# Slot ids fetched one block earlier, and a narrow block's rows turned in the last two steps of the block ahead

## The chip, the core and the metric

The kernel runs on one core of one Trainium2 chip. Its engines run side by side, each with a queue of its own: TensorE (PE: matrix products, and transposes written as products with the identity), VectorE (DVE), ScalarE (ACT), GpSimd (POOL, which here issues the indirect transfers) and SyncE (SP, which issues the plain loads). The metric is the device time of one execution in microseconds (us); less is better.

## The reference, cut to what matters

A layer first mixes 2048 tokens of width 1024 and normalises them; that part is not touched. Then comes a mixture of experts: every token picks a group and two of its eight experts, out of 32 in all. The changed code computes this (biases and the sorting are left out):

```python
def hier_moe(t, ...):                                    # t: (2048, 1024)
    g_val, g_idx = top_k(softmax(t @ rg_w), 1)
    e_val, e_idx = top_k(in_group(t @ re_w, g_idx), 2)
    weights = g_val * softmax(e_val)
    for each expert e:
        xb = the rows of t that chose e                  # gathered by slot id
        hid = silu(xb @ w1[e]) * (xb @ w3[e])            # 1024 -> 512
        y[rows of xb] += weights * (hid @ w2[e])         # 512 -> 1024
```

After it a second layer norm writes the output.

## The kernel before

The span has three stages: the mixer up to 1350 us, the experts from there to 2161.5 us, and the last norm. The router writes, for each expert, a list of slots into `idxD` in device memory: a slot holds a token's row number and its weight. An expert `e` owns `LE` slots there. `u2D` holds the rows to gather, `accD` the sum that the outputs are added to.

**Blocks.** The experts are ranked by size and worked off in 33 blocks. Block 0 holds 128 rows of the largest. Then wide blocks (`Wide`, 144 to 224 rows, odd numbers 1 to 27) alternate with narrow ones (`Block`, 80 to 128 rows, even numbers 2 to 28), and blocks 29 to 32 are four more narrow ones. A wide block has its rows in two halves. All products of 32-bit numbers are made as three products of a high and a low part.

**Rows of a block.** `gather` first loads the slots into a small tile `ix` (SP's queue, L1322), then has POOL fetch the token rows into `X` by them (an indirect transfer, L1324). `X` has three buffers, `ix` eight. `turned` (L1330) transposes four columns of 128 of `X` on TensorE into a PSUM tile `ptx`, of which there are two; `split_rows` then makes the high part on ScalarE (L1334) and the low part on VectorE (L1335), as `xw` (wide) or `xx` (narrow). A narrow block takes two such turns, a wide one four.

**Weights.** A piece of 512 KB is loaded by SP into one of eight buffers `raw` (L1307); `split` makes `whi` on ScalarE (L1314) and `wlo` on VectorE (L1315). A piece's buffer is free again, and the next load can be issued, when its `wlo` is done. `pump(m)` does up to m splits and issues the loads that follow. Each expert has eight pieces for the up products and four for the down products.

**Order.** Everything is issued in the order of the code, and each engine takes its own part of it in that order. Block t goes through four steps `s_`: its up products (L1395 to L1397 narrow, L1452 and L1453 wide), turns of block t + 1 (a wide one in each step, a narrow one in steps 0 and 2), two splits, and in step 0 `prepare(t + 2)`. `finish` is a block's down products (L1341 to L1343) and `put`, which scales the result on VectorE (`y`, L1350) and has POOL add it to `accD` (L1351). It comes in step 1 of the next block for a narrow one; a wide block finishes its first half at its own end, its second half at the end of the next block.

Of the kernel before, what the change touches and what calls it, by code (L numbers as in the profile page):

```python
# [10 lines left out]
I32 = mybir.dt.int32  # L11
# [63 lines left out]
def hymba_kernel(ctx, tc, xT, ctxT, x, small, rows, ada_w, w_in, gate_w, w_out, router_w, w1, w3, w2, out):  # L75
# [606 lines left out]
    slots = []  # L682
# [62 lines left out]
    for si in range(len(slots), 3, -1):  # L745
        a, b, c, d = slots[si - 4:si]
        turn = si == len(slots) or slots[si][0] != d[0] or (si - 4 > 0 and slots[si - 5][0] != a[0])
# [157 lines left out]
    with ExitStack() as st:  # L905
# [204 lines left out]
        def place(i):  # L1110
# [5 lines left out]
            sl = fs.tile([128, 2], F32, name="sl")  # L1116
            dve.tensor_reduce(sl, ho, axis=AX.X, op=ALU.add)
            dve.scalar_tensor_tensor(dest[:, i, :], ee, float(LE), sl, op0=ALU.mult, op1=ALU.add)
# [10 lines left out]
        def choose():  # L1129
# [11 lines left out]
            sp.dma_start(lead_ix, idxD[bass.ds(e * LE, 128), :])  # L1141
            X = upool.tile([128, D], F32, name="X0", tag="wr", bufs=2)
            pool.indirect_dma_start(out=X, out_offset=None, in_=u2D, in_offset=bass.IndirectOffsetOnAxis(ap=lead_ix[:, 0:1], axis=0))
            return e, X

        def turn_lead(X):
            pts = []
# [140 lines left out]
    with ExitStack() as st:  # L1288
# [5 lines left out]
        ex = st.enter_context(tc.tile_pool(name="ex", bufs=2))  # L1294
# [21 lines left out]
            k = 4 if n < 8 else 2  # L1316
            return [t.rearrange("p (k c) -> p k c", k=k) for t in (hi, lo)]

        def gather(row, n):

            ix = ex.tile([128, 2], I32, name="ix", tag="ix", bufs=8)
            sp.dma_start(ix[:n], idxD[bass.ds(row, n), :])  # L1322
            X = ex.tile([128, D], F32, name="X", tag="X", bufs=3)
            pool.indirect_dma_start(out=X[:n], out_offset=None, in_=u2D, in_offset=bass.IndirectOffsetOnAxis(ap=ix[:n, 0:1], axis=0))  # L1324
            return ix, X

        def turned(X, n, k0):
            pt = psT.tile([128, 4, 128], F32, name="ptx", tag="pt")
            for k in range(4):
                pe.transpose(pt[:, k, :n], X[:n, 128 * (k0 + k):128 * (k0 + k) + 128], ident[:n, :n])  # L1330
            return pt[:, :, :n]

        def split_rows(xh, xl, pt):
            act.copy(xh, pt)  # L1334
            dve.tensor_sub(xl, pt, xh.bitcast(F32))  # L1335
# [9 lines left out]
        def put(py, ix, n):  # L1345

            y = ex.tile([128, D], F32, name="y", tag="y")
            for nh in range(2):
                s = slice(512 * nh, 512 * nh + 512)
                dve.scalar_tensor_tensor(y[:n, s], py[nh][:n], ix[:n, 1:2].bitcast(F32), g2[:n, s], op0=ALU.mult, op1=ALU.mult)  # L1350
            pool.indirect_dma_start(out=accD, out_offset=bass.IndirectOffsetOnAxis(ap=ix[:n, 0:1], axis=0), in_=y[:n], in_offset=None, compute_op=ALU.add)  # L1351
# [4 lines left out]
        class Block:  # L1356
# [3 lines left out]
            def __init__(self, row, n, weights, slot):  # L1360
                self.row, self.n, self.w, self.slot = row, n, weights, slot

            def gather(self):
                self.ix, self.X = gather(self.row, self.n)

            def places(self):
                x = ex.tile([128, KC, 2, 128], F32R, name="xx", tag=self.slot, bufs=1)
# [11 lines left out]
            def turn(self, i):  # L1379
                if i == 0:  # L1380
                    self.places()
                k0 = 4 * i
                split_rows(self.xh[:, k0:k0 + 4, :], self.xl[:, k0:k0 + 4, :], turned(self.X, self.n, k0))
# [32 lines left out]
            def put(self, part=0):  # L1416
                put(self.py, self.ix, self.n)
# [3 lines left out]
        class Wide:  # L1421
# [5 lines left out]
            def __init__(self, row, n, weights, slot):  # L1427
                self.row, self.n, self.m, self.w, self.slot = row, n, n // 2, weights, slot

            def gather(self):  # L1430
                self.src = [gather(self.row + self.m * a, self.m) for a in range(2)]

            def turn(self, i):
                n, m = self.n, self.m
                if i == 0:
                    self.x = ex.tile([128, KC, 2, n], F32R, name="xw", tag=self.slot, bufs=1)
                a, k0 = i // 2, 4 * (i % 2)
                s = slice(m * a, m * a + m)
                split_rows(self.x[:, k0:k0 + 4, 0, s], self.x[:, k0:k0 + 4, 1, s], turned(self.src[a][1], m, k0))

            def up(self, s, kk):

# [29 lines left out]
                down(self.hh[:, k, s], self.hl[:, k, s], self.w[8 + k], k, self.py, self.m)  # L1472

            def put(self, part):
                put(self.py, self.src[part][0], self.m)

        SP = (mybir.EngineType.SP,)
        SPP = (mybir.EngineType.SP, mybir.EngineType.Pool)
# [17 lines left out]
        nb = len(blocks)  # L1496
        wide = [n > 128 for _, _, n, _ in blocks] + [False]

        def reg(s_):
            if s_ not in regs:  # L1500
                regs[s_] = nc.values_load(etab[0:1, sched[s_]:sched[s_] + 1], engines=SP, min_val=0, max_val=31)
            return regs[s_]
# [27 lines left out]
        if True:  # L1530
            B = []
            rest = overflow()

            def prepare(t):
                if t < nb:
                    s_, o, n, _ = blocks[t]
                    slot = "xw" if wide[t] or (not wide[t - 1] and B[t - 1].slot == "xs") else "xs"
                    B.append((Wide if wide[t] else Block)(reg(s_) * LE + o, n, weights[s_], slot))
                    B[t].gather()

            def finish(t, part):
                for k in range(4):
                    while 8 + k not in B[t].w:
                        pump(1)
                    B[t].down(k, part)
                    if blocks[t][3] and part == B[t].parts - 1:
                        state["down"] += 1
                    pump(1)
                B[t].put(part)

            def turn(t, i):
                if t < nb and i < B[t].turns:
                    B[t].turn(i)

            def used(t, i):
                if blocks[t][3]:
                    state["up"] += 2

            def late(t):
                if t == nb // 2:  # L1560
                    sp.dma_start(l2b, rows[0:1, 4096 + 3 * D:4096 + 4 * D].to_broadcast([128, D]))


            fetch_to(2)
            B.append(Block(reg(0) * LE, 128, weights[0], "xs"))
            prepare(1)
            prepare(2)
            fetch_to(NRAW)
            B[0].lead(lead_ix, lead_pt)
            pump(4)  # L1570
            for t in range(nb):
                for s_ in range(4):
                    while 2 * s_ + 1 not in B[t].w:
                        pump(1)
                    if wide[t]:
                        for kk in range(4):
                            B[t].up(s_, kk)
                            if kk == 1:
                                pump(1)
                    else:  # L1580
                        B[t].up(s_)
                    used(t, s_)
                    if s_ % 2 and wide[t]:
                        B[t].hidden(s_ // 2)
                    if s_ == 3 and not wide[t]:
                        B[t].hidden()
                    if s_ == 0 and t and not wide[t - 1]:
                        B[t - 1].turn_hidden()
                    if t + 1 < nb and wide[t + 1]:
                        turn(t + 1, s_)  # L1590
                    elif s_ % 2 == 0:
                        turn(t + 1, s_ // 2)
                    pump(2)
                    if s_ == 0:
                        if t:
                            prepare(t + 2)
                        late(t)
                    if s_ == 2 and t:
                        next(rest, 0)
                    if s_ == 1 and t and not wide[t - 1]:  # L1600
                        finish(t - 1, 0)
                    if s_ == 3 and t and wide[t - 1]:
                        finish(t - 1, 1)
                    if s_ == 3 and wide[t]:
                        finish(t, 0)
            B[nb - 1].turn_hidden()
            finish(nb - 1, 0)
# [4 lines left out]
        with tc.For_i(0, nov) as i:  # L1612
            oe = ex.tile([1, 2], I32, name="oe", tag="oe")
            for k in range(2):
                sp.dma_start(oe[:, k:k + 1], otD[0:1, bass.ds(i + k * (NOV + 2), 1)])
            e = nc.values_load(oe[0:1, 0:1], engines=ENG, min_val=0, max_val=31)
            row = nc.values_load(oe[0:1, 1:2], engines=ENG, min_val=0, max_val=32 * LE - 128)
            b = Block(row, 128, {}, "xs")
            b.gather()
            b.turn(0)  # L1620
            b.turn(1)
            for n in range(12):
                b.w[n] = split(fetch(e, n), n)
            for s_ in range(4):
                b.up(s_)
            b.hidden()
            b.turn_hidden()
            for k in range(4):
                b.down(k)
            b.put()  # L1630
# [98 lines left out]
```

## Time and profile before

| | |
|---|---|
| time, median of 3 runs | 2242.07 us (2241.68 to 2252.21) |
| profiled execution | 2243.1 us, span 2241.0 us from the first to the last instruction |
| busy share of the span | PE 91%, DVE 76%, ACT 52%, POOL 31% |
| mean granted TensorE clock | 0.957 of full speed |
| up to 1350 us | PE 1263.23 us busy, DMA share 0.42 |
| experts, 1350 to 2161.5 us | PE 776.79 us busy of 811.5, DMA share 0.90, 293 GB/s |
| last norm, to 2241 us | PE 8.31 us busy of 79.5 |

The profiled execution is 1.0 us above the median of the runs. "DMA share" is the mean busy share of the core's 16 DMA engines. Expert weights make up most of what is moved in the middle stage.

### The profile page before, as it was taken

What the parts mean: (1) busy time and instruction counts of PE and PEld (TensorE: products, weight loads), DVE (VectorE), ACT (ScalarE), POOL (GpSimd) and SP (SyncE); (2) the same over time, 40 slices, a digit from 0 to 9 for tenths busy, and PEclk for the clock granted to TensorE, in tenths of its full rate; (3) what the DMA queues carried; (4) which work ended last, traced back from release to release, by engine and by line L of the source; (5) the groups of instructions that cost most, each with busy time, mean ns of one, the idle gap of its engine ahead of it and who ended that gap; (6) DMA issues with size and microseconds to landing.
All of it is one profiled execution on the core that took longest, in us unless ns stands there. A gap on an engine that the chain in (4) does not pass through costs nothing. (4 is left out here: it accounts for less than half of the span.)

```text
span 2241.0 us, 34527 instructions
## 1 busy us (share of the span) xinstructions
PE 2048.3 (91%) x12440; PEld 1810.6 (81%) x12440; DVE 1713.6 (76%) x2632; ACT 1167.9 (52%) x1863; POOL 700.3 (31%) x532
## 2 busy tenths in 40 slices
PE   7999998999998999989799987999999999999960
PEld 3788778999997988889588877888888888788850
DVE  6677776866866888888677875788877788787869
ACT  3456554644655545535444324566665666565633
POOL 5121142222333232231466661112222223222116
PEclk9999999999999999999899987999999999999985
DMA  8324333323334144244765527899998989898965
GB/s 267 107 102 138 105 127 129 131 94 123 105 100 153 58 162 145 70 149 165 263 206 174 158 78 277 245 294 303 294 303 276 306 295 299 286 310 301 334 215 237
DMA packets 180515, 441.56 MB, mean 197 GB/s; under 512 B 27365, under 2 KB 69349, under 8 KB 179830
## 3 DMA queue, kind: packets, MB, share of 16 engines
q1 hardware_dynamic: 155446, 385.18, 49.6%
q0 software_dynamic: 15088, 46.81, 8.5%
q10 hardware_dynamic: 9808, 7.34, 1.0%
q8 instruction: 99, 1.62, 0.3%
q14 instruction: 74, 0.61, 0.1%
HBM read 358.63 MB, written 80.63 MB: 196 GB/s over the span
## 5 line engine op out<-in xcount | busy, mean ns | idle before, releaser
L1315 DVE TENSOR_TENSOR wlo<-raw,whi 128x1024 fp32r<-128x1024 f32 x384 | 452.3, 1220 | 55.4 <-ACT whi L1314 51.0
L356 PE MATMUL pp<-uh,wh 128*128 128x384 f32 (+2 forms) x1248 | 445.5, 357 | 4.6 <-ACT uh L246 2.3
L357 PE MATMUL pp<-ul,wh 128*128 128x384 f32 (+2 forms) x1248 | 429.1, 344 | 4.8 <-DVE ul L247 4.6
L358 PE MATMUL pp<-uh,wl 128*128 128x384 f32 (+2 forms) x1248 | 427.6, 343 | 3.0 <-DVE wl L247 3.0
L1314 ACT CAST whi<-raw 128x1024 fp32r<-128x1024 f32 x384 | 382.5, 1050 | 38.8 <-PE pye L1342 23.1
L1452 PE MATMUL ph<-xw,whi 128*128 128x448 f32 (+3 forms) x896 | 259.6, 365 | 1.6 <-DVE hid L1403 1.6
L356 PEld LDWEIGHTS pp<-uh,wh 128*128 128x128 f32 x1248 | 238.5, 191 | 26.3 <-ACT rgs L614 5.9
L357 PEld LDWEIGHTS pp<-ul,wh 128*128 128x128 f32 x1248 | 238.4, 191 | 19.8 <-DVE ul L247 10.3
L358 PEld LDWEIGHTS pp<-uh,wl 128*128 128x128 f32 x1248 | 237.5, 190 | 13.4 <-DVE wl L247 4.6
L1453 PE MATMUL ph<-xw,wlo 128*128 128x224 f32 (+3 forms) x896 | 222.3, 248 | 0.0
L388 POOL TENSOR_SCALAR mraw<-mraw,sil 128x512 f32<-128x512 f32 x56 | 99.7, 1780 | 363.1 <-DMA mraw<-in_ada_w_dram 363.1
L1351 POOL DMA_INDIRECT accD<-y,ix x46 | 113.1, 2459 | 316.5 <-DVE y L1350 315.9
L1452 PEld LDWEIGHTS ph<-xw,whi 128*128 128x128 f32 x896 | 174.7, 195 | 7.2 <-DVE hid L1403 1.8
L1395 PE MATMUL ph<-whi,xx 128*80 128x256 f32 (+3 forms) x608 | 175.3, 288 | 3.7 <-ACT whi L1314 3.5
L1453 PEld LDWEIGHTS ph<-xw,wlo 128*128 128x128 f32 x896 | 177.2, 198 | 1.2
L1397 PE MATMUL ph<-wlo,xx 128*80 128x256 f32 (+3 forms) x608 | 172.2, 283 | 1.4 <-DVE wlo L1315 1.4
L1396 PE MATMUL ph<-whi,xx 128*80 128x256 f32 (+3 forms) x608 | 171.6, 282 | 0.0
L1324 POOL DMA_INDIRECT X<-u2D,ix x46 | 65.5, 1425 | 320.8 <-PE pye L1343 134.3
L489 PE MATMUL pa<-Q,km 128*128 128x128 f32 x896 | 124.0, 288 | 19.2 <-DVE Q L492 11.9
L489 PEld LDWEIGHTS pa<-Q,km 128*128 128x128 f32 x896 | 118.4, 193 | 25.1 <-ACT K L419 7.0
L247 DVE TENSOR_TENSOR wl<-wr,wh 128x1024 fp32r<-128x1024 f32 x84 | 109.7, 1306 | 34.8 <-ACT wh L246 34.7
L490 DVE COPY_PREDICATED A<-masks,pa 128x384 f32<-128x384 uint8 (+1 forms) x140 | 84.1, 618 | 46.9 <-PE pa L489 44.1
(350 smaller groups left out, 4566.7 us busy)
## 6 DMA issues: line engine op xcount, KB each, us to landing
raw<-in_w_dram SPq DMA_DIRECT2D x384, 512.0 KB
wr<-in_w_in_dram SPq DMA_DIRECT2D x84, 512.0 KB
mraw<-in_ada_w_dram SPq DMA_DIRECT2D x64, 256.0 KB
aw<-in_ada_w_dram SPq DMA_DIRECT2D x16, 512.0 KB
fx<-in_x_dram SPq DMA_DIRECT2D x16, 512.0 KB
accD<-fr SPq DMA_DIRECT2D x16, 512.0 KB
u2D<-fu SPq DMA_DIRECT2D x16, 512.0 KB
f<-accD SPq DMA_DIRECT2D x16, 512.0 KB
```

The lines of the kernel that those rows point to most:

```text
L356: pe.matmul(ps, wh[:, k, :], uh[:, k, :], start=k == 0, stop=False)
L357: pe.matmul(ps, wh[:, k, :], ul[:, k, :], start=False, stop=False)
L358: pe.matmul(ps, wl[:, k, :], uh[:, k, :], start=False, stop=k == KC - 1)
L489: pe.matmul(pa[:, c, :], km[:, s:s + 128], cut(Q, s, [(2 * b, 64 // b), (T + b, 2), (1, b)]), start=True, stop=True)
L1314: act.copy(hi, raw)
L1315: dve.tensor_sub(lo, raw, hi.bitcast(F32))
L1351: pool.indirect_dma_start(out=accD, out_offset=bass.IndirectOffsetOnAxis(ap=ix[:n, 0:1], axis=0), in_=y[:n], in_offset=None, compute_op=AL ...
L1395: pe.matmul(p, self.xh[:, k, :], wh[:, kk, :], start=k + g == 0, stop=False, skip_group_check=True)
L1396: pe.matmul(p, self.xl[:, k, :], wh[:, kk, :], start=False, stop=False, skip_group_check=True)
L1397: pe.matmul(p, self.xh[:, k, :], wl[:, kk, :], start=False, stop=k == KC - 1, skip_group_check=True)
L1452: pe.matmul(p[:, :2 * n], wh[:, kk, f], self.x[:, k].rearrange("p h t -> p (h t)"), start=k == 0, stop=False)
L1453: pe.matmul(p[:, :n], wl[:, kk, f], self.x[:, k, 0, :], start=False, stop=k == KC - 1)
```

## The change

The load of the slots becomes a method of its own, `slots`, and `prepare` is cut in two: `place(t)` makes a block and loads its slots, `prepare(t)` gathers the rows of block t and places block t + 1. So the slots of block t + 2 are asked for where those of block t + 1 were. `ix` gets a ninth buffer. Before the first block, blocks 1 to 3 are placed now. Apart from that, a narrow block's two turns go from steps 0 and 2 of the block ahead of it to steps 2 and 3. No product, transfer or cast is added or left out.

```diff
-        def gather(row, n):
+        def slots_of(row, n):
-            ix = ex.tile([128, 2], I32, name="ix", tag="ix", bufs=8)
+            ix = ex.tile([128, 2], I32, name="ix", tag="ix", bufs=9)
             sp.dma_start(ix[:n], idxD[bass.ds(row, n), :])
+            return ix
+        def gather(ix, n):
             X = ex.tile([128, D], F32, name="X", tag="X", bufs=3)
             pool.indirect_dma_start(out=X[:n], out_offset=None, in_=u2D, in_offset=bass.IndirectOffsetOnAxis(ap=ix[:n, 0:1], axis=0))
-            return ix, X
+            return X
...
             def prepare(t):
                 if t < nb:
+                    B[t].gather()
+                place(t + 1)
+            def place(t):
+                if len(B) <= t < nb:
                     s_, o, n, _ = blocks[t]
                     slot = "xw" if wide[t] or (not wide[t - 1] and B[t - 1].slot == "xs") else "xs"
                     B.append((Wide if wide[t] else Block)(reg(s_) * LE + o, n, weights[s_], slot))
-                    B[t].gather()
+                    B[t].slots()
...
             fetch_to(2)
             B.append(Block(reg(0) * LE, 128, weights[0], "xs"))
+            place(1)
+            place(2)
             prepare(1)
             prepare(2)
             fetch_to(NRAW)
...
                     if t + 1 < nb and wide[t + 1]:
                         turn(t + 1, s_)
-                    elif s_ % 2 == 0:
-                        turn(t + 1, s_ // 2)
+                    elif s_ >= 2:
+                        turn(t + 1, s_ - 2)
```

What this does to TensorE's queue, after step 0 of a wide block of 144 rows that a narrow block of 112 rows follows (`hid` is the hidden layer of the narrow block ahead, `X` the rows of the narrow block to come). Before:

```order
L1452 MATMUL ph_18583<-xw_18392,whi_18400 128x288
L1453 MATMUL ph_18583<-xw_18392,wlo_18401 128x144
L1330 MATMUL ptx_18623<-ident_88,hid_18518 128x112 x4
L1330 MATMUL ptx_18631<-ident_88,X_18424 128x112 x4
L1452 MATMUL ph_18582<-xw_18392,whi_18406 128x288
```

The same place now, and below it, from the same block, its end, where the down products of its first half begin:

```order
L1462 MATMUL ph_18597<-xw_18404,whi_18412 128x288
L1463 MATMUL ph_18597<-xw_18404,wlo_18413 128x144
L1334 MATMUL ptx_18637<-ident_88,hid_18532 128x112 x4
L1462 MATMUL ph_18596<-xw_18404,whi_18418 128x288
L1463 MATMUL ph_18596<-xw_18404,wlo_18419 128x144
```

```order
L1462 MATMUL ph_18775<-xw_18404,whi_18688 128x288
L1463 MATMUL ph_18775<-xw_18404,wlo_18689 128x144
L1334 MATMUL ptx_18881<-ident_88,X_18424 128x112 x4
L1345 MATMUL pye_18900<-whi_18728,hw_18710 72x512
L1346 MATMUL pye_18900<-whi_18728,hw_18710 72x512
```

The first turn of `X` is gone from step 0 (it stands in step 2 now), and the second stands ahead of the down products at the end of the block, where there was none.

SP's queue ahead of the first block, between the slots of blocks 1 and 2 and the third piece of weights (a `TENSOR_LOAD` reads an expert's number into a register). Before:

```order
L1322 DMA ix_12103<-idxD_68 80x2
L1501 TENSOR_LOAD etab_155
L1501 ISA x2
L1322 ISA
L1322 DMA ix_12117<-idxD_68 80x2
L1307 ISA
L1307 DMA raw_12121<-in_w1_dram 128x1024
```

Now:

```order
L1322 DMA ix_12113<-idxD_68 80x2
L1511 TENSOR_LOAD etab_155
L1511 ISA x2
L1322 ISA
L1322 DMA ix_12131<-idxD_68 112x2
L1322 ISA
L1322 DMA ix_12133<-idxD_68 112x2
L1307 ISA
L1307 DMA raw_12135<-in_w1_dram 128x1024
```

One register load and the two slot loads of block 3 have come in ahead of the third piece. POOL's queue has the same order as before.

## Rows read from the trace of the kernel before

**Rows 1.** Waits of PE from 1400 to 2161.5 us: total us, times, longest.

```profile
PE ptx L1330 <- DMA X<-u2D,ix: 19.3, 9, 4.4
```

**Rows 2.** Windows: length, busy us of each engine, PE clock, DMA share, GB/s.

```profile
1400.00:2161.50 761.50, 736.72 (x4942) 645.58 (x4941) 607.35 (x704) 463.00 (x598) 172.59 (x87) 0.98 0.90 294
```

**Rows 3.** Timeline of PE, turns of narrow blocks: start, us; in brackets the wait ahead.

```profile
1739.59 0.47 PE L1330 MATMUL ptx<-ident,X 80*128 80x80 f32 x4 [1.44 <-DMA X<-u2D,ix]
...
1754.18 0.44 PE L1330 MATMUL ptx<-ident,X 80*128 80x80 f32 x4
...
2104.69 0.63 PE L1330 MATMUL ptx<-ident,X 128*128 128x128 f32 x4 [1.11 <-DMA X<-u2D,ix]
2116.36 0.60 PE L1330 MATMUL ptx<-ident,X 128*128 128x128 f32 x4
2124.51 0.63 PE L1330 MATMUL ptx<-ident,X 128*128 128x128 f32 x4 [1.35 <-DMA X<-u2D,ix]
```

**Rows 4.** Chain that ended last, 1720 to 1740 us: start, us, what.

```profile
1720.92 2.28 DVE wlo L1315 x2
...
1724.59 7.51 DMA ix<-idxD
...
1732.92 6.53 DMA X<-u2D,ix
```

**Rows 5.** Timeline of POOL, 1719 to 1741 us.

```profile
1720.79 3.86 POOL L1351 DMA_INDIRECT accD<-y,ix  x1 [13.76 <-DVE y L1350]
1732.92 0.95 POOL L1324 DMA_INDIRECT X<-u2D,ix  x1 [8.28 <-PE pye L1343]
```

**Rows 6.** Windows behind four of the waits, columns as in rows 2.

```profile
1687.50:1694.50 7.00, 6.99 (x32) 7.00 (x33) 3.98 (x4) 3.26 (x4) 0.00 (x0) 0.55 0.77 224
1789.00:1793.00 4.00, 3.96 (x21) 4.00 (x21) 2.52 (x3) 3.26 (x4) 0.00 (x0) 0.57 0.89 290
1936.90:1942.00 5.10, 5.02 (x23) 5.05 (x24) 3.12 (x4) 3.37 (x4) 0.00 (x0) 0.50 0.45 112
2037.60:2043.00 5.40, 5.31 (x28) 5.34 (x29) 3.32 (x4) 3.42 (x4) 0.00 (x0) 0.60 0.47 123
```

**Rows 7.** Timeline of PE, up products of one wide block after a wait.

```profile
1790.30 0.55 PE L1452 MATMUL ph<-xw,whi 128*128 128x320 f32 x1
...
1790.78 0.55 PE L1452 MATMUL ph<-xw,whi 128*128 128x320 f32 x1
...
1793.25 0.34 PE L1452 MATMUL ph<-xw,whi 128*128 128x320 f32 x1
...
1793.51 0.35 PE L1452 MATMUL ph<-xw,whi 128*128 128x320 f32 x1
```

**Rows 8.** Chain that ended last, start of the experts, columns as in rows 4.

```profile
1354.78 0.33 SPq L1322
...
1356.45 0.35 SPq L1307
...
1371.54 0.39 PE ph L1397
```

**Rows 9.** Windows of a pair, of the stretch behind it, of a late narrow block.

```profile
1636.00:1684.00 48.00, 47.90 (x329) 41.82 (x329) 40.03 (x47) 30.28 (x40) 13.60 (x7) 1.00 0.96 310
1684.00:2085.00 401.00, 382.01 (x2583) 331.75 (x2582) 314.18 (x366) 240.80 (x317) 101.36 (x47) 0.97 0.90 295
2098.00:2118.00 20.00, 18.89 (x138) 17.72 (x138) 18.17 (x19) 14.26 (x18) 2.90 (x3) 1.00 1.03 387
```

**Rows 10.** Timeline, end of a wide block into the narrow one behind it.

```profile
1761.64 0.53 DVE L1335 TENSOR_TENSOR hw<-hidw,hw 128x352 fp32r<-128x352 f32 x1 [0.55 <-ACT hw L1334]
...
1767.80 0.32 PE L1395 MATMUL ph<-whi,xx 128*80 128x256 f32 x1
```

**Rows 11.** Timeline, end of a late narrow block into the next narrow one.

```profile
2120.84 0.68 DVE L1403 TENSOR_TENSOR hid<-hid,ph 128x512 f32<-128x512 f32 x1
...
2122.56 0.60 PE L1330 MATMUL ptx<-ident,hid 128*128 128x128 f32 x4
```

More of the change, by code (lines that the diff above doesn't have):

```diff
@@ L1361, in __init__, with slots @@
                 self.row, self.n, self.w, self.slot = row, n, weights, slot
+            def slots(self):
+                self.ix = slots_of(self.row, self.n)
             def gather(self):
-                self.ix, self.X = gather(self.row, self.n)
+                self.X = gather(self.ix, self.n)
             def places(self):
@@ L1428, in __init__, with slots @@
                 self.row, self.n, self.m, self.w, self.slot = row, n, n // 2, weights, slot
+            def slots(self):
+                self.ix = [slots_of(self.row + self.m * a, self.m) for a in range(2)]
             def gather(self):
-                self.src = [gather(self.row + self.m * a, self.m) for a in range(2)]
+                self.X = [gather(ix, self.m) for ix in self.ix]
             def turn(self, i):
@@ L1438, in turn @@
                 s = slice(m * a, m * a + m)
-                split_rows(self.x[:, k0:k0 + 4, 0, s], self.x[:, k0:k0 + 4, 1, s], turned(self.src[a][1], m, k0))
+                split_rows(self.x[:, k0:k0 + 4, 0, s], self.x[:, k0:k0 + 4, 1, s], turned(self.X[a], m, k0))
             def up(self, s, kk):
@@ L1474, in put @@
             def put(self, part):
-                put(self.py, self.src[part][0], self.m)
+                put(self.py, self.ix[part], self.m)
         SP = (mybir.EngineType.SP,)
@@ L1618, in hymba_kernel @@
             b = Block(row, 128, {}, "xs")
+            b.slots()
             b.gather()
```

## Prediction

> **What bounds the kernel now.** I read the windows of the three stages first. The change touches only the experts, and there TensorE is the bound: from 1400 to 2161.5 us it is busy for 736.72 of 761.5 us [rows 2], so at most 24.8 us of idle time can go, plus what a lowered clock costs. The view of waits then says for what PE stood still: 19.3 us, in 9 waits, for gathered rows `X` that had not landed when PE came to transpose them [rows 1]. In the timeline every one of these waits stands ahead of a narrow block's first turn, in step 0 of the block ahead; three of them are shown. The second turn, 14.6 us later between wide and narrow (1754.18), finds its rows [rows 3]. No turn of a wide block waits.
>
> The chain of waits says why the rows are late [rows 4]. SP can issue a load of weights only when the split ahead has freed a buffer; the slots' load is queued behind such loads, so it goes out at 1724.59 us, right after a pair of `wlo`. It needs 7.51 us to land, and the gather behind it 6.53 us, and the second cannot start before the first has landed: PE, which wants the rows at 1739.59 - 1.44 = 1738.15 [rows 3], goes on at 1739.59.
>
> **The change part by part.** *Slots one block earlier.* The slots' load keeps its places in SP's queue, but what is loaded there is now for the block after. So the gather no longer waits for it. What is late next for the gather is POOL's own queue: the addition ahead of it ends at 1720.79 + 3.86 = 1724.65 us [rows 5], so the gather goes out at about 1725 instead of 1732.92 and lands, at the same 6.53 us, near 1731.5. The buffer of `X` that it fills was emptied a block before, also after the move of the turns. That is 8 us earlier, and the longest of the nine waits is 4.4 us.
>
> *The turn moved.* The first turn of a narrow block goes to where its second was, and that is 14.6 us later in a wide block [rows 3]. By itself this is also more than the longest wait. In the last blocks, where narrow follows narrow, it is 2116.36 - 2104.69 = 11.7 us. So each part alone covers the waits, and I count all of them: **-19.3 us** (between 0, if something else is as late, and 24.8).
>
> *The clock.* After four of the nine waits PE went on at a lower level: in the windows behind them the granted clock is 0.55, 0.57, 0.50 and 0.60 [rows 6]. Of the two levels, 1.2 and 2.4 GHz, that makes 2 x (7.0 x 0.45 + 4.0 x 0.43 + 5.1 x 0.50 + 5.4 x 0.40) = 19.2 us at the lower one. What PE loses there I take from the spacing of its up products: 0.48 us a pair at the lower level, 0.26 us at the upper [rows 7], so 1 - 0.26 / 0.48 = 0.46 of the time, 19.2 x 0.46 = 8.8 us. With the waits gone, nothing lowers the clock: **-8.8 us**. (The Trainium skill, "TensorE: Matmul & The Clock Gate", section Terms, puts the penalty at the throttled time times one minus the granted share, which is half of it; by it an estimate of 9.6 us would stand here, and the sum would be -26.0 us. The rows show a little less, and the sum goes by them.)
>
> *The start.* SP gets one register load and two slot loads more ahead of the third piece of weights. The same three things stand in the chain between 1354.78 and 1356.45 us [rows 8]: 1.67 us. Here nothing hides them, since the chain runs from there through the weights to PE, which waits for them up to 1371.54. **+1.7 us**, between 0 and twice that.
>
> *The last blocks.* Two of the nine waits, 1.11 and 1.35 us [rows 3], lie where the DMA engines are full (share 1.03, 387 GB/s [rows 9]). There the weights may be late instead, so I give back half: **+1.2 us** (0 to 2.5).
>
> *Split of the moved turn.* One cast on ScalarE and one subtraction on VectorE go from step 0 to step 2, one of each from step 2 to step 3. In step 3 they stand behind `hw`, which VectorE ends at 1761.64 + 0.53 = 1762.17 us; half a us later the low part of `xx` is ready, near 1762.7. The next block reads this half first at 1767.80 [rows 10], after the down products and its own first step. That cover is 5 us; without it each us would be paid 14 times. In the four last narrow blocks the cover is thinner: the hidden layer's product ends at 2121.52 us, the low part would follow at 2122.2, and the turn of `hid`, behind which it is wanted, begins at 2122.56 [rows 11]; 0.4 to 1 us. I count 0, with up to 4 us as a bound. PE's own transposes are as many as before. On ScalarE the cast that stood in step 0 no longer holds up the weight casts behind it; no gain is counted for that.
>
> The ninth `ix` buffer adds no wait: the wide and narrow pairs take three buffers each, so a buffer comes round after three pairs, about 150 us.
>
> Sum: -19.3 - 8.8 + 1.7 + 1.2 = **-25.2 us**, made against the profiled execution, 2243.1 us, which lies 1.0 us above the median of the runs. So 2217.9 us for a profiled execution and **2217 us** for the median. Its own range, from the bounds of the last four terms, is 2213 to 2224.
>
> **Rivals.**
>
> *The DMA engines take over.* From 1684 to 2085 us the DMA share is 0.90 over 401 us, so 361 us of work [rows 9]. My forecast takes 19.3 - 2.5 = 16.8 us of waits and 8.8 us of clock out of this stretch; the same work in 375 us is a share of 0.96. For it speaks that the stage as a whole runs at 0.90 [rows 2], near to full. Against it: the pair of blocks from 1636 to 1684 us runs at exactly 0.96, with PE busy for 47.90 of 48.00 us [rows 9], and behind the waits the share falls to 0.45 to 0.89 [rows 6], so the DMA engines stood idle because PE did. If no more than 0.93 could be held, midway between 0.90 and 0.96, the stretch would need 361 / 0.93 = 388 us, 13 us less than now; with the start's 1.7 us and nothing from the last blocks that is 2242.1 - 11.3 = **2231 us**. The Trainium skill, "DMA: Bandwidth & Descriptors", section "Issuing engines are not separate DMA queues", speaks for this rival: transfers of SP and POOL run on the same 16 engines and interleave, so an earlier gather takes its share from the weights. The trace agrees in that both are slow together (7.51 and 6.53 us for small transfers).
>
> *Another wait comes up.* The stops of PE may have let ScalarE and VectorE catch up with the weights; then PE would wait for `wlo` or `hw` instead. Outside the waits for `X` PE's idle time is 24.8 - 19.3 = 5.5 us, and in the pair from 1636 to 1684 us, where nothing stops PE, ScalarE and VectorE keep up (40.03 of 48 us busy on VectorE [rows 9]), which speaks against it. If two thirds of the 28.1 us came back like this, the time would be **2236 us**. That the gather is late for another reason than its slots, so that the first part does nothing, comes out like the forecast, since the moved turn covers it alone.
>
> *Slower.* The second turn in step 3 could come too late for the narrow block: its split waits behind VectorE's queue, PE stops in every narrow block. It decides at 2.0 us in each of 18 blocks, since 18 x 2.0 is the 25.2 us gained plus the 11.2 us that make 0.5%; with a cover of 5 us the low part must come 7 us later than worked out. At 7.5 us it would be 18 x 2.5 = 45 us, less 25 gained: **2262 us**. The order of the queues speaks against it: nothing but `hw` stands between.
>
> **How the numbers follow.** Forecast 0.75; DMA 0.13; another wait 0.07; slower 0.05. The predicted time is that of the forecast, 2217. The range goes from 2209 (all 24.8 us of idle time and 8.8 of clock gone, 2242.1 - 33.6) to 2231 (the DMA rival), which leaves out the last two. A measurement of this kernel tells 0.5%, 11.2 us, from no change, so faster means below 2230.9: the forecast, and half of the DMA rival, together 0.81; within 0.5%: the other half and the third case, 0.14; slower 0.05.
>
> **What would show it.** In the view of waits the row of PE for `X` should be gone after 1400 us. The clock should be 1.00 in all windows from 1400 to 2161.5, which should take about 735 us. POOL should issue a narrow block's gather within 1 us of the end of the addition ahead. The first PE product that waits on weights near 1371.5 should move by 1.7 us. I am wrong if PE waits for `wlo`, `xx` or `hw` in the pairs, or if ScalarE waits for `raw` in them (DMA).

## The result, and the profile after

The changed kernel takes 2216.07 us (median of 4 runs, 2215.42 to 2218.6); the kernel before, beside it, 2247.14 us. The ratio on record is 0.9881, with a 95% interval from 0.9852 to 0.9911: faster, and within 1 us of the 2217 forecast. The profiled execution takes 2215.94 us, 27.2 less than the one of before. That is the better figure for the gain than the 31 us between the two medians, since the four runs of before lie 12 us apart.

PE's waits, in the kernel after, from 1400 to 2136 us (total us, times, longest). They answer to [rows 1]. Neither 2136 nor the 2161.5 us of before is quite the end of the experts: both lie in the down products of the last block, whose addition POOL issues at 2140.29 us after and 2167.10 before.

```profile
PE ptx L1334 <- DVE hid L1410: 1.4, 1, 1.4
PE pye L1345 <- ACT hw L1338: 1.0, 1, 1.0
PE pye L1346 <- DVE hw L1339: 0.7, 4, 0.2
PE pye L1345 <- ACT hx L1338: 0.7, 1, 0.7
PE pye L1346 <- DVE hx L1339: 0.2, 1, 0.2
```

The row for `X` is gone, and nothing has taken its place: 4.0 us of small waits are left, 4.5 beside the waits for `X` before. POOL's timeline after, at the place of [rows 5], shows the gather following the addition ahead by 0.30 us, where 8.28 us lay between them:

```profile
1718.77 3.86 POOL L1355 DMA_INDIRECT accD<-y,ix  x1 [13.70 <-DVE y L1354]
1722.93 0.95 POOL L1328 DMA_INDIRECT X<-u2D,ix  x1 [0.30 <-PE ptx L1334]
```

To compare the stages without the shift of the start, I cut both profiles at the same additions of POOL: from block 1's to the 18th of all, from there over eight wide and narrow pairs to the 42nd, and over the last narrow blocks to the 46th. The windows of before between these marks (length, busy us of PE, PEld, DVE, ACT, POOL, then PE clock, DMA share, GB/s):

```profile
1411.09:1683.76 272.67, 271.65 (x1790) 238.03 (x1789) 217.74 (x257) 165.41 (x213) 61.04 (x33) 1.00 0.90 289
1683.76:2085.74 401.98, 382.99 (x2591) 332.73 (x2591) 314.85 (x366) 241.20 (x318) 101.59 (x47) 0.97 0.90 295
2085.74:2155.34 69.60, 67.14 (x476) 62.89 (x475) 64.49 (x65) 49.49 (x57) 8.40 (x6) 1.00 0.92 328
```

The same three after, ahead of them the whole stage (as in [rows 2]) and behind them a piece of the last blocks (as in [rows 9]):

```profile
1400.00:2136.00 736.00, 731.68 (x4985) 643.96 (x4985) 607.08 (x707) 462.64 (x599) 174.88 (x88) 1.00 0.94 304
...
1415.45:1687.80 272.35, 271.66 (x1789) 239.74 (x1788) 217.65 (x257) 165.40 (x213) 55.87 (x34) 1.00 0.92 291
1687.80:2061.39 373.59, 372.27 (x2591) 324.05 (x2590) 313.49 (x366) 239.63 (x318) 107.02 (x47) 1.00 0.98 317
2061.39:2129.51 68.12, 68.12 (x486) 63.69 (x485) 64.49 (x65) 50.19 (x57) 8.80 (x7) 1.00 0.92 335
...
2073.00:2093.50 20.50, 20.50 (x154) 19.41 (x152) 18.11 (x20) 16.29 (x19) 2.74 (x2) 1.00 1.03 387
```

The gain lies in the pairs: 401.98 - 373.59 = 28.4 us. It has two parts, and the columns split them. PE's idle time falls from 401.98 - 382.99 = 19.0 us to 1.3. And PE's busy time for the same 2591 products falls from 382.99 to 372.27, by 10.7 us: that goes with the lower level of the clock, whose mean over this stretch is 0.97 before and 1.00 after. The stretch ahead of the pairs gains 0.3 us. The last blocks gain 1.5, but between these two additions PE makes 476 products before and 486 after. Up to the last addition, the 47th, there are 517 in both, and the gain is 2.46 us; first before, then after:

```profile
2085.74:2167.10 81.36, 75.51 (x517) 69.25 (x515) 67.30 (x69) 50.67 (x59) 9.95 (x8) 1.00 0.83 287
2061.39:2140.29 78.90, 75.52 (x517) 68.95 (x515) 67.32 (x69) 51.37 (x59) 10.36 (x8) 1.00 0.84 296
```

The start, from the last write of slots into `idxD` (1349.77 us before, 1352.05 after) to block 1's addition, is longer, 63.40 us instead of 61.32. SP's queue shows 1.65 us of it; after, at the place of [rows 8], it takes 3.87 us from the first slot load to the third piece of weights, where it took 2.22:

```profile
1356.53 3.68 SPq L1322 DMA_DIRECT2D ix<-idxD  x5
1360.40 4.04 SPq L1307 DMA_DIRECT2D raw<-in_w_dram  x7
```

### The profile page after: what moved, and what is told of

It is laid out like the page before. It is cut to its first block, busy times and chain, and to the rows that moved or that the text cites. A ratio compares the mean times of both kernels' runs of the same rounds, so it can differ in the third digit from the quotient of the medians.

```text
span 2214.1 us, 34509 instructions
## 1 busy us (share of the span) xinstructions
PE 2039.9 (92%) x12440; PEld 1806.3 (82%) x12440; DVE 1707.8 (77%) x2632; ACT 1167.5 (53%) x1863; POOL 703.8 (32%) x532
## 5 line engine op out<-in xcount | busy, mean ns | idle before, releaser
L357 PEld LDWEIGHTS pp<-ul,wh 128*128 128x128 f32 x1248 | 239.0, 191 | 19.3 <-DVE ul L247 9.8
L358 PEld LDWEIGHTS pp<-uh,wl 128*128 128x128 f32 x1248 | 238.6, 191 | 15.9 <-DVE wl L247 7.0
L1462 PE MATMUL ph<-xw,whi 128*128 128x448 f32 (+3 forms) x896 | 249.7, 354 | 1.6 <-DVE hid L1410 1.6
L1462 PEld LDWEIGHTS ph<-xw,whi 128*128 128x128 f32 x896 | 168.3, 188 | 7.2 <-DVE hid L1410 1.8
L1463 PEld LDWEIGHTS ph<-xw,wlo 128*128 128x128 f32 x896 | 171.1, 191 | 1.2
L1001 PE MATMUL py<-woh,mh 128*128 128x512 f32 x256 | 113.8, 445 | 1.9 <-ACT mh L985 1.9
```

The lines of the kernel that those rows point to most:

```text
L357: pe.matmul(ps, wh[:, k, :], ul[:, k, :], start=False, stop=False)
L358: pe.matmul(ps, wl[:, k, :], uh[:, k, :], start=False, stop=k == KC - 1)
L1462: pe.matmul(p[:, :2 * n], wh[:, kk, f], self.x[:, k].rearrange("p h t -> p (h t)"), start=k == 0, stop=False)
L1463: pe.matmul(p[:, :n], wl[:, kk, f], self.x[:, k, 0, :], start=False, stop=k == KC - 1)
```

## The experiments

The theory: PE's waits for late rows, and the lowered clock behind them, cost 28 us, and each of the two parts removes them alone. The rivals: one part does it all, the DMA engines are the next bound, or the moved turn has a price of its own. The first four kernels shared one chip and one set of runs of before (median 2241.16 us), the next four another (2240.22), the last three a third (2246.48). "Start", "first", "pairs", "last" are the stretches above in the profiled execution of each, cut at the same marks ("last" up to the 46th addition); "experts" goes from the last write of slots to the last addition, with 5208 products in each kernel. The mixer, which no kernel changes, ends at 1349.27 to 1357.88 us in these executions (by the last write of slots), so a few us between two medians say little; the experts as a whole repeat to 1 us (after and 9, 2 and 10, 7 and 11 are the same kernels).

| kernel | median us (range) | ratio to before (95%) | start | first | pairs | last | experts |
|---|---|---|---|---|---|---|---|
| before | 2242.07 (2241.68 to 2252.21) | | 61.32 | 272.67 | 401.98 | 69.60 | 817.33 |
| after | 2216.07 (2215.42 to 2218.6) | 0.9881 (0.9852 to 0.9911) | 63.40 | 272.35 | 373.59 | 68.12 | 788.24 |
| 1 early slots alone | 2219.39 (2218.77 to 2223.44) | 0.99 (0.9871 to 0.9929) | 62.45 | 273.85 | 375.41 | 68.57 | 792.74 |
| 2 moved turn alone | 2211.95 (2210.43 to 2213.85) | 0.9862 (0.9834 to 0.9891) | 62.50 | 271.29 | 371.87 | 68.12 | 784.33 |
| 3 block 3's slots later | 2214.12 (2211.62 to 2219.39) | 0.9876 (0.9846 to 0.9905) | 62.03 | 272.80 | 373.24 | 68.23 | 788.14 |
| 4 both turns last | 2214.86 (2214.32 to 2220.01) | 0.9876 (0.9839 to 0.9914) | 62.58 | 271.15 | 371.42 | 70.60 | 789.20 |
| 5 gather a step later | 2276.62 (2271.27 to 2284.2) | 1.0161 (1.012 to 1.0201) | 61.66 | 271.58 | 419.89 | 76.18 | 842.57 |
| 6 more loads | 2222.39 (2219.32 to 2227.68) | 0.991 (0.9876 to 0.9944) | 63.90 | 273.71 | 377.86 | 70.65 | 795.78 |
| 7 moved turn, weights first | 2209.7 (2206.62 to 2215.0) | 0.9866 (0.9836 to 0.9895) | 58.72 | 271.28 | 371.96 | 68.66 | 781.17 |
| 8 moved turn, four pieces first | 2213.8 (2212.69 to 2218.91) | 0.9877 (0.9848 to 0.9905) | 62.02 | 271.28 | 372.14 | 69.67 | 785.76 |
| 9 both parts again | 2218.32 (2214.67 to 2220.8) | 0.9875 (0.9847 to 0.9903) | 63.86 | 272.40 | 373.07 | 67.73 | 788.35 |
| 10 moved turn alone again | 2212.4 (2209.01 to 2217.38) | 0.9848 (0.9821 to 0.9876) | 61.64 | 271.28 | 371.98 | 67.34 | 783.44 |
| 11 as 7, again | 2211.91 (2209.79 to 2212.33) | 0.9851 (0.9824 to 0.9878) | 58.78 | 271.04 | 372.09 | 68.28 | 780.66 |

**1. The early slots alone.** The kernel after, with the turns back in steps 0 and 2:

```diff
-                    elif s_ >= 2:
-                        turn(t + 1, s_ - 2)
+                    elif s_ % 2 == 0:
+                        turn(t + 1, s_ // 2)
```

> Slots one block earlier, the turns of a narrow block back in steps 0 and 2. Theory (each part alone covers the waits): the gather goes out right behind POOL's addition, 7 to 8 us earlier, and the longest wait was 4.4 us, so no wait of PE for X over 0.5 us after 1400 us, clock 1.00 there, and 2216 to 2218 us. Rival (the early gather lands late all the same, because it shares the DMA engines with the weights, and the moved turn did the work): waits for X of 8 to 12 us in all remain and the clock falls behind some of them, 2226 to 2234 us.

2219.39 us, 1.4 above the upper end of what was expected. No wait for `X` after 1400 us; POOL's gather goes out 0.30 us behind the addition, as with both parts. So the early slots suffice alone to remove these waits.

**2. The moved turn alone.** The kernel before, with the same edit the other way round:

```diff
-                    elif s_ % 2 == 0:
-                        turn(t + 1, s_ // 2)
+                    elif s_ >= 2:
+                        turn(t + 1, s_ - 2)
```

> The turns of a narrow block in steps 2 and 3, the slots loaded where they were before. Theory: the first turn comes 11 to 15 us later than the rows were wanted, so no wait of PE for X after 1400 us; the start is as before, so it saves the 1.7 to 2.1 us that the extra loads cost there: 2214 to 2215 us. Rival (without the early slots ScalarE and VectorE still run behind SP's late loads, or the rows of wide blocks become late next): 2220 us or more, with waits for X in step 0 of the narrow blocks.

2211.95 us, 2 below what was expected, again with no wait for `X` after 1400 us, although its gather is still late. POOL's timeline of this kernel, at the place of [rows 5]:

```profile
1718.57 5.43 POOL L1351 DMA_INDIRECT accD<-y,ix  x1 [11.66 <-DVE y L1350]
1728.17 1.57 POOL L1324 DMA_INDIRECT X<-u2D,ix  x1 [4.18 <-PE pye L1342]
```

POOL still stands 4.18 us between the addition and the gather, and nobody waits for that. So each part alone removes all waits for `X`; and the second adds nothing to SP's queue at the start, while both together are no faster than it alone. The two are not worth the same, though. Kernels 1 and 2 shared a chip, their ranges don't touch, and the experts take 792.74 us in the one and 784.33 in the other. Nothing of that lies in the start (62.45 and 62.50 us); 2.6 us lie in the first stretch, 3.5 in the pairs and 2.4 in the last blocks. In the pairs PE waits 1.9 us for `hw` in kernel 1 and not at all in kernel 2, and is busy for 372.95 us instead of 371.50. What makes the rest was not found.

**3. Block 3's slots behind the weights.** The kernel after, with the loads that it adds at the start moved behind the weights:

```diff
             prepare(1)
-            prepare(2)
+            B[2].gather()
             fetch_to(NRAW)
+            place(3)
```

> The changed kernel with one thing moved: the register load and the two slot loads of block 3 come behind the first eight loads of weights. Theory (they cost the start 1.7 us and no more): from the last scatter of slots to the third load of weights 6.7 us again instead of 8.35, and 2214 us, 1.7 to 2.1 us less than the changed kernel. Rival (the start is paced by the DMA engines or by the wait for block 1's rows, the loads are hidden): 2216 us, no less.

SP is back to 2.22 us between the first slot load and the third piece (1355.12 to 1357.34 us), and the start takes 62.03 us instead of 63.40. The median, 2214.12 us, is 2 us lower than the change's own, which lies inside the spread of the runs; the stretch shows 1.4 us of gain, the total does not prove it, and the experts as a whole take 788.14 us, as with the change.

**4. Both turns in the last step.** The kernel after, so that the split of both halves stands behind `hw`:

```diff
-                    elif s_ >= 2:
-                        turn(t + 1, s_ - 2)
+                    elif s_ == 3:
+                        turn(t + 1, 0)
+                        turn(t + 1, 1)
```

> The changed kernel with both turns of a narrow block in step 3. Theory (cover of 5 us behind a wide block, almost none behind a narrow one): the 14 narrow blocks behind a wide one still find their rows split, PE waits there less than 0.5 us each; the four last ones need the first half at once and wait about 2 us each for xx: 2222 to 2228 us. Rival (the cover is thinner than worked out, since the splits queue behind the weights on VectorE): PE waits 2 us or more for xx in all 18 blocks, over 36 us, 2250 us or more.

A miss to the good side: 2214.86 us, no slower than the change. The waits of PE in this kernel, same stretch:

```profile
PE ph L1403 <- DVE xx L1339: 1.4, 3, 0.5
PE ph L1402 <- ACT xx L1338: 0.9, 3, 0.3
```

2.3 us in six waits, all of them in the last narrow blocks, whose stretch grows from 68.12 to 70.60 us. In the pairs there is none for `xx`. The cover of the moved turn is thus real in the pairs, and thin only where narrow follows narrow, where the change itself, with one turn in step 3, waits for nothing.

**5. The gather a step later.** The kernel before made worse, to price the waits: `prepare` goes from step 0 to step 1.

```diff
+                    if s_ == 1 and t:
+                        prepare(t + 2)
                     if s_ == 0:
-                        if t:
-                            prepare(t + 2)
                         late(t)
```

> The kernel before with prepare (slots and gather) in step 1 instead of step 0, so that the rows come later and PE waits longer. Both theories expect more than the 19.3 us of waits for X after 1400 us. Theory (a wait costs its length, and where the clock falls behind it half of the time at the lower level on top): the stages from 1411 us to the last addition take as long as in the changed kernel, 714 us, plus the waits, plus half of the time at the lower level, each read from this run's trace, within 4 us. Rival (the clock costs nothing of its own, since PE would wait for the weights or the DMA engines anyway): 714 us plus the waits alone.

2276.62 us, 1.6% slower than before. First the row of its waits from 1400 to 2200 us, then its windows over all three stretches and over the pairs:

```profile
PE ptx L1330 <- DMA X<-u2D,ix: 34.2, 11, 5.8
```

```profile
1419.24:2186.89 767.65, 728.65 (x4828) 639.46 (x4827) 597.90 (x687) 455.78 (x586) 170.26 (x86) 0.97 0.88 287
1690.82:2110.71 419.89, 388.20 (x2585) 337.39 (x2583) 315.60 (x366) 241.52 (x318) 100.14 (x48) 0.96 0.87 282
```

The three stretches together take 767.65 us instead of 714.06 after (272.35 + 373.59 + 68.12). PE is idle for 39.0 us of that, 37 more than after, and busy for 728.65 instead of 712.05, 16.6 more, for the same products. So a wait was paid for twice here, once as itself and then by the clock: 34.2 us of waits for `X`, 37 us of idle time in all, made 53.6 us. The rival, by which the waits alone set the time, falls: it gives 714 + 34.2 = 748 us. The theory's sum, with half of the time at the lower level in the pairs (16.8) and the last blocks (3.0) on top, gives 768, within its 4 us.

**6. More loads.** The kernel after, with 384 KB more per block, loaded into a buffer that nothing reads:

```diff
                         late(t)
+                        extra = ex.tile([128, 768], F32, name="extra", tag="extra", bufs=1)
+                        sp.dma_start(extra, w2[0, 0:128, 0:768])
```

> The changed kernel with one more load of 384 KB in each of the 33 blocks, into a buffer that nothing reads: 0.79 MB more to a pair of blocks, 6% of its weights. Theory (at a share of 0.98 the DMA engines still have some room, since 1.03 was seen): the stretch of pairs takes 0 to 8 us more, 2216 to 2225 us. Rival (0.98 is already the limit, the gain ended there): 33 x 0.39 MB at about 320 GB/s are 41 us more, and PE waits for weights, 2250 us or more.

2222.39 us, 6 us above the change. The windows of the pairs in this kernel, then the waits of SP's queue in them:

```profile
1693.73:2071.59 377.86, 373.04 (x2591) 324.02 (x2590) 313.89 (x366) 240.15 (x318) 107.02 (x48) 1.00 1.00 330
```

```profile
SPq L1307 <- DVE wlo L1315: 208.4, 163, 5.4
SPq L1307 <- DMA raw<-in_w_dram: 12.2, 9, 2.7
```

The DMA engines carry 330 GB/s here, 330 x 377.86 - 317 x 373.59 = 6.3 MB more in the pairs, which is the 16 extra loads, at a share of 1.00; the pairs take 4.3 us longer. Now SP waits for loads on the way, which it doesn't do in the pairs after; PE's waits for `hw` there grow from 1.0 to 4.5 us, and ScalarE's for `raw` from 1.6 to 6.9. So the DMA engines are not the bound after the change, but at a share of 0.98 they are close to it: this little more is where they begin to be.

**7. The moved turn, with weights ahead of block 2's slots.** Since the turn suffices, the version with the shortest start: kernel 2 and

```diff
             prepare(1)
-            prepare(2)
             fetch_to(NRAW)
+            prepare(2)
```

> The moved turn alone, with block 2's slots and gather behind the first eight loads of weights. Theory (the start is paced by the third to eighth load of weights): these go out one register load and one slot load, 1.3 us, earlier against the last scatter, 5.4 us instead of 6.7, and the time is 1 us under that of the moved turn alone, 2211. Rival (the start is paced by the rows of block 1): no difference, 2212.

2209.7 us, the lowest median of the study. SP asks for the third piece 5.75 us after the last write of slots (1349.27 to 1355.02), 6.79 in kernel 2, and the start takes 58.72 us instead of 62.50. That is 3.8 us less, where 1 us was expected. About 2 us of it is PE's busy time for the same 318 products; the windows of the start, of kernel 2 and then of 7:

```profile
1353.64:1416.14 62.50, 50.69 (x318) 46.10 (x319) 37.52 (x49) 29.75 (x40) 7.15 (x8) 0.82 0.83 275
1349.27:1407.99 58.72, 48.69 (x318) 44.33 (x319) 37.53 (x49) 29.58 (x40) 7.16 (x7) 0.84 0.86 292
```

The edit also moves block 2's gather back (POOL issues it 20.6 us behind the last write of slots, 9.7 in kernel 2); the two were not tried apart.

**8. Four pieces ahead of all slots.** Kernel 7, with `fetch_to(4)` for `fetch_to(2)`:

```diff
-            fetch_to(2)
+            fetch_to(4)
             B.append(Block(reg(0) * LE, 128, weights[0], "xs"))
             prepare(1)
             fetch_to(NRAW)
             prepare(2)
```

> As the run before, and four loads of weights ahead of the slots instead of two. Theory: PE's second step then has its weights, the other loads go out as before with less ahead of them, so 2 to 4 us less than the moved turn alone, 2208 to 2210. Rival (the slots of block 1 queue behind 2 MB of weights and their rows come 3 to 5 us later, so PE waits for X instead): 2212 to 2215.

Too far, as the rival said: 2213.8 us, and the start takes 62.02 us. The waits of PE at the start (1350 to 1400 us) have the rows of block 1 first:

```profile
PE ptx L1330 <- DMA X<-u2D,ix: 7.2, 1, 7.2
PE ph L1395 <- ACT whi L1314: 3.7, 1, 3.7
```

In kernel 7 that wait is 4.0 us. The slots' load has fallen behind two more pieces of weights.

**9 to 11. Both parts, the turn alone, and kernel 7 side by side.** The kernels are those of after, 2 and 7, unchanged.

> The change as it stands, on one chip with the two runs that have only the moved turn. Theory: each part alone covers the waits, so the early slots add nothing to the moved turn and cost 1.7 us at the start; this run is 1.5 to 4 us slower than the moved turn alone, and its pairs of blocks take the same to within 1 us. Rival: the earlier gather also costs something in the pairs (it takes its share of the DMA engines while weights are due); then the pairs take 1.5 us or more longer than with the moved turn alone, as they did once (373.59 against 371.87), and the whole is 3 to 5 us slower.

> The moved turn alone, unchanged, on the same chip. Theory: 1.5 to 4 us faster than both parts together, all of it ahead of the first pair; pairs of blocks like those of both parts to within 1 us. Rival: 3 to 5 us faster, 1.5 us or more of it in the pairs.

> The moved turn, with the weights' pieces asked for ahead of block 2's slots, on the same chip. If the start is paced by the third piece of weights, which is asked for 5.4 us earlier here, it is 1.5 to 4 us faster than the moved turn alone; if block 1's rows or the second layer of waits behind them pace it, the two are within 1 us. Against both parts together 3 to 7 us faster, or 1.5 to 4.

The turn alone has a median 5.9 us below both parts together, more than either side expected, though the ranges overlap. The experts take 788.35 us in kernel 9 and 783.44 in kernel 10; the first time it was 788.24 and 784.33. Of these 4.9 us 63.86 - 61.64 = 2.2 us lie at the start and 713.20 - 710.60 = 2.6 us in the three stretches. The windows of the pairs, first of kernel 9, then of 10:

```profile
1693.07:2066.14 373.07, 372.27 (x2591) 324.00 (x2590) 313.61 (x366) 239.64 (x318) 107.04 (x47) 1.00 0.98 317
```

```profile
1690.80:2062.78 371.98, 371.57 (x2591) 323.21 (x2590) 313.69 (x366) 239.95 (x318) 113.69 (x48) 1.00 0.96 319
```

The pairs differ by 1.1 us, just above what the theory allowed and under the rival's 1.5. That the earlier gather costs time there isn't borne out either: kernel 4, which has the early slots too, took 371.42 us. What makes the 1 to 2 us, most of it in how long PE is busy, stays open. Kernel 11 against 10: the start is 2.9 us shorter, as in kernel 7, and the experts are 2.8 us shorter, but the medians are only 0.5 us apart. The 5.4 us of the expectation were wrong: it compared moments of two executions that had reached the experts at different times. Counted from the last write of slots, the third piece is asked for 5.44 us after it instead of 6.67, so 1.2 us earlier.

## Why the prediction was right

Term by term, against the profiled executions:

- **The waits, -19.3.** Right. The row for `X` is gone, with nothing in its place. That each part alone covers the waits was said from 8 us and 14.6 us of lead; kernels 1 and 2 show it.
- **The clock, -8.8.** Right in kind, and too small by 2 us: PE's busy time over the pairs fell by 10.7. I had added up the windows behind four waits [rows 6]; the third of them ended before the lower level did, as the window behind it shows:

```profile
1942.00:1943.00 1.00, 1.00 (x6) 1.00 (x6) 1.00 (x1) 0.00 (x0) 0.00 (x0) 0.53 0.83 287
```

That adds 0.94 us at the lower level, or 0.4 us at the price of 0.46. The other 1.5 us stay open. The price came from the spacing of one block's products, and the busy time of the same 2591 products differs by 2 us between kernels that have a clock of 1.00 in the pairs (370.73 us in kernel 4, 372.95 in kernel 1). The better way was one step longer: the busy time of the same products with and without the loss. By the Trainium skill, "TensorE: Matmul & The Clock Gate", section Terms, half of the throttled time is lost; an estimate with the mean clock 0.97 over 401.98 us gives 12.1 us, or 10.0 to 14.1 with the rounding. The trace agrees within the rounding, with 10.7 us here and, in kernel 5, where 0.96 over 419.89 us gives 16.8, with 388.20 - 372.27 = 15.9 us.
- **The start, +1.7.** About right. SP's part is 3.87 - 2.22 = 1.65 us, as worked out; the start as a whole is 2.1 us longer, 2.2 in kernel 9 against 10. Kernel 3 takes 1.4 of it back, though its experts as a whole are no shorter (788.14 us). A single start is not exact to 1 us either: kernels 2 and 10 are the same and have 62.50 and 61.64. With block 3's slots ahead of the weights (after, 1, 4, 6, 9) it takes 62.45 to 63.90 us, without them (before, 2, 3, 10) 61.32 to 62.50, and the means are 1.4 us apart. The sign named for this term failed: the last product of block 0 that waits for weights starts at 1371.69 us, 19.6 us behind the last write of slots instead of 21.8. PE has waited for weights at earlier places by then, and the mean granted clock of the start is 0.80 instead of 0.84.
- **The last blocks, +1.2.** Wrong: it should have been 0. I gave back half of 2.5 us because the DMA engines are full there. With the same 517 products the blocks became 2.46 us shorter, which is both waits, 1.11 and 1.35 us, in full. PE waits for nothing in the piece with a share of 1.03 and 387 GB/s.
- **The split, 0.** Right. In the timeline after, at the place of [rows 10], the low part follows `hw` and is done at 1758.43 us; the next block's products begin 2.3 us later, and those of its second step, which read this half, 5.3 us later, against the 5 us worked out:

```profile
1757.51 0.53 DVE L1339 TENSOR_TENSOR hw<-hidw,hw 128x352 fp32r<-128x352 f32 x1 [0.55 <-ACT hw L1338]
1757.95 0.48 DVE L1339 TENSOR_TENSOR xx<-ptx,xx 128x320 fp32r<-128x320 f32 x1
...
1760.70 0.28 PE L1402 MATMUL ph<-whi,xx 128*80 128x256 f32 x1
...
1763.74 0.32 PE L1402 MATMUL ph<-whi,xx 128*80 128x256 f32 x1
```

Where I saw 0.4 to 1 us of cover, in the last blocks, kernel 4 had to put a second turn there before PE waited at all.

The sum, -25.2, stands against -27.2 measured. The experts alone became 29.1 us shorter (817.33 to 788.24): pairs -28.4, first stretch -0.3, last blocks -2.5, start +2.1. The rest is mainly the mixer, which ran 2.3 us longer in this execution and which the change doesn't touch. So the mechanism was right, but that the time came within 1 us is partly luck: the terms fall 3.9 us short (idle time and clock by 3, the last blocks by 1.2), and the mixer hid more than half of that. The lower end of the forecast's own range should have read 2214, not 2213: without its three costs the sum is -28.1.

Of the signs of being wrong two are there to the letter: in the pairs PE waits once for `hw`, 1.0 us, and ScalarE twice for `raw`, 1.6 us. Before it was 1.5 and 3.9 us, so neither is a new bound.

Of the rivals, the DMA engines came nearest. The forecast put their share at 0.96, and the rival said that no more than 0.93 could be held; the trace has 0.98 with PE busy for 372.27 of 373.59 us. So its threshold was wrong, by the pair at 0.96 [rows 9] that already stood against it, but its direction wasn't: kernel 6 reaches it with 4.3 us in the pairs. No other wait came up, and the slower case would have needed waits for `xx`, of which the change has none after 1400 us.

What the prediction did not ask is whether both parts are worth having. Since it had each cover the waits alone, and gave a price to the early slots only, the moved turn alone was the better kernel by its own sum, by 1.7 us. The medians say 4 to 6 us, the stage of the experts 3.9 and 4.9; of the 4.9 the start makes 2.2, and the rest is unexplained.

## What to carry to other kernels

When data comes late, look first at whether the consumer can ask later in its own queue, where other work covers it: that needs no extra buffer and no place in another queue, while fetching earlier costs something wherever nothing ahead hides it, here at the start. Price a wait of TensorE by its busy time too: here the lowered clock added about half as much again (10.7 us to 17.7 us of idle time in the pairs before, 16.6 to 37 in kernel 5). And before removing waits from a stage that already moves data 90% of the time, work out the share that the shorter stage will need, and measure with a few extra loads how far the reserve goes.

## What the runs showed of the hardware

- The busy share of the DMA engines is not in step with the bytes. If a share of 1 is taken as full, at 0.98 over 373.59 us some 7.5 us were free (5.6 to 9.3 with the rounding); the 16 extra loads of kernel 6 took these and 4.3 us more, about 12 us, where 16 x 393216 bytes at the 317 GB/s of the stretch would need 19.8.
- A share of 1.03 (387 GB/s, 20.5 us in the last blocks) left PE without one wait, so a share of 1 by itself doesn't say that the DMA engines are the bound.
- In the start a few small loads weigh more than their bytes. With one register load and two slot loads more (3.87 against 2.22 us in SP's queue) block 1's addition came 1.4 us later in the mean (five profiled executions with them, four without). With a register load, a slot load and the gather behind it less ahead of the weights (kernels 7 and 11) it came 2.9 to 3.8 us earlier, more than the 1.0 to 1.2 us by which the weights were asked for earlier. About 2 us of that is PE's busy time for the same products; what makes it was not tried apart.
